# The low levels of a chunked recurrence on halves of the matmul array

## The chip, the cores and the metric

One Trainium2 chip, one core of it. The metric is the device time of one execution in microseconds, the median of several. The core has a matmul engine (TensorE, PE in the profile, with its weight loads as PEld), VectorE (DVE), ScalarE (ACT), GpSimd (POOL) and a DMA-issuing engine (SP). Each works through its own instructions in order and waits on semaphores for the others.

## The reference

One layer of a decoder: 256 tokens, width 1024, all in fp32. A normed input goes through one wide projection into nine parts; two of them feed an attention branch, four a gated linear recurrence (HGRN2), and the branches are merged, followed by cross attention to 256 memory tokens and a feed-forward block. The change lies in the recurrence, which for 8 heads of key width 128 is

```python
qh = silu(heads(q, dk)) * (dk ** -0.5)
fg = lbh + (1.0 - lbh) * sigmoid(heads(f, dk))
kh = 1.0 - fg
...                                    # b = cumsum(log fg) within a chunk
diff = b[:, :, :, None, :] - b[:, :, None, :, :]
decay = where(causal, exp(diff), 0.0)
a = einsum('bhtd,bhsd,bhtsd->bhts', qc, kc, decay)
o = o_inter + einsum('bhts,bhsv->bhtv', a, vc)
```

So for each head a causal 256 x 256 matrix is wanted, whose entry (t, s) is the sum over d of q(t, d) k(s, d) times the product of the forget gates between s and t.

## The kernel before

**Products.** Every large product is made in three parts, hi x hi, hi x lo and lo x hi (L280 to L282). A weight chunk of 1 MB is read by DMA (raw), ScalarE makes hi of it (L211) and VectorE lo = raw - hi (L212). There are three buffers each of hi and lo, and chunks are prepared up to two ahead. `gemm_t` works off two chunks, the two halves of the contraction, for 512 columns; each half takes some 5.5 us of TensorE.

**The recurrence matrix by levels.** For each head and each of two blocks of 128 tokens (16 blocks, index a = 2 x head + block) the kernel keeps the keys `KS[:, a]` and the queries `QP[:, a]`, with the 128 key dimensions on the partitions, and fills the block of the matrix `at3[:, a]` (keys on the partitions, queries along the free axis). This is done level by level: at level L the tokens are seen in groups of 2L, and the later half's queries meet the earlier half's keys. `widen` multiplies queries and keys by the gates of their group, so that they serve the next level. Level one multiplies all keys by the even queries (`QQ`), and a mask leaves the diagonal. Levels 2 and 4 share one product, and so do 8 and 16: `pair_queries` writes the queries in three pieces of 64 into `QQ` (for levels 2 and 4 the fourth piece holds the odd queries), `pair_levels` multiplies all 128 keys by them, and VectorE copies what belongs into `at3` under masks (`lm`). At level 32, 64 and 128 `level` multiplies just the keys and queries that meet. An fp32 product of this kind is one call and two instructions in the trace.

**What sets the order.** TensorE's order is that of the program text. `hgrn` is a generator that is advanced by one `yield` at each tick, and there is a tick after each half of a `gemm_t` or `gemm_f`. So one stretch of recurrence matmuls stands between two halves of a projection: the value projection of the recurrence (`Vb`), that of the attention (`va`), its rotated queries and its rotated keys. The order of VectorE, ScalarE and GpSimd is found by a scheduler when the kernel is built, except for GpSimd's early part, which is in the order of the text. The 16 blocks are handled as two groups g of 8 (heads 0 to 3 and 4 to 7): stretches with 4 blocks each at levels 1 to 16, with 8 each from level 32 on.

**PSUM.** `bank` takes one of four banks of the pool `sm`; the projections take theirs from the four of the pool `mm`. The last step of the query projection (`ev_q`) makes `QQ` for one head at a time: an add and a product on VectorE, Silu on ScalarE (L529) and the copy into `QQ` on ScalarE (L534).

Of the kernel before, what the change touches and what calls it, by code (L numbers as in the profile page):

```python
# [13 lines left out]
AF = mybir.ActivationFunctionType  # L14
ALU = mybir.AluOpType
# [112 lines left out]
def bc(ap, n, axis):  # L128
    shape = list(ap.shape)
    shape.insert(axis, n)  # L130
    return ap.unsqueeze(axis).to_broadcast(shape)


def build(tc, A, out):
    nc = tc.nc
    V, SC, G, PE, SY = nc.vector, nc.scalar, nc.gpsimd, nc.tensor, nc.sync
    with ExitStack() as ctx:
# [11 lines left out]
        def big(tag, name, shape=(128, 8, 256), dt=F32):  # L149
            return bp.tile(list(shape), dt, name=name, tag=tag)  # L150
# [15 lines left out]
        def bank(name, shape=(128, 512)):  # L166
            return sm.tile(list(shape), F32, name=name, tag="sm")
# [3 lines left out]
        lm = cp.tile([128, 448], I32, name="lm")  # L171
# [294 lines left out]
        l0, l1 = gv[:, V_L0:V_L0 + 8], gv[:, V_L1:V_L1 + 8]  # L466
# [13 lines left out]
        QQ = [big(tag, "QQ", (128, 8, 256)) for tag in ("B6", "B6b")]  # L480
# [77 lines left out]
        w = by_k(nxt(), 4)  # L558
# [7 lines left out]
        QP, KS = QK[:, 0], QK[:, 1]  # L566
# [8 lines left out]
        w = by_k(nxt(), 4)  # L575
# [31 lines left out]
        def by_parity(a0, w):  # L607
            return at3[:, a0:a0 + 2].rearrange("p a (j w) -> p a j w", w=2)[:, :, :, w]

        def level_one(g, bs):  # L610
            for b in bs:
                a0 = 8 * g + 2 * b
                ps = bank("l1", (128, 2, 64))
                for j in range(2):
                    PE.matmul(ps[:, j], KS[:, a0 + j], QQ[g][:, a0 + j - 8 * g, 0:64], start=True, stop=True)
                V.tensor_tensor(by_parity(a0, 0), ps, bc(ident2[:, :, 0], 2, 1), op=ALU.mult)

        def widen(g, L, parts="qkt"):
            ga = slice(8 * g, 8 * g + 8)
            T1 = tview(L, g).rearrange("p a (i w) -> p a i w", w=2)  # L620
            T0, Tq = T1[:, :, :, 0], T1[:, :, :, 1]
            if L < 64:
                _, qs = blocks(QP[:, ga], L)
                kf, _ = blocks(KS[:, ga], L)
                n = 64 // L
                if "q" in parts:
                    V.tensor_tensor(qs, qs, T0.unsqueeze(3).to_broadcast([128, 8, n, L]), op=ALU.mult)
                if "k" in parts:
                    V.tensor_tensor(kf, kf, Tq.unsqueeze(3).to_broadcast([128, 8, n, L]), op=ALU.mult)
                if "t" in parts:  # L630
                    G.tensor_tensor(tview(2 * L, g), T0, Tq, op=ALU.mult)
# [22 lines left out]
        def pair_levels(g, L, bs):  # L654
            for b in bs:
                a0 = 8 * g + 2 * b
                n = 256 if L == 2 else 192
                ps = bank("lp", (128, 2, n))
                for j in range(2):
                    PE.matmul(ps[:, j], KS[:, a0 + j], QQ[g][:, a0 + j - 8 * g, 0:n], start=True, stop=True)  # L660
                if L == 2:
                    V.tensor_tensor(by_parity(a0, 1), ps[:, :, 192:256], bc(two_rows, 2, 1), op=ALU.mult)
                for i in range(3):
                    M = L if i == 0 else 2 * L
                    li = (1 if L == 2 else 4) + i
                    mask = lm[:, 64 * li:64 * li + 64].rearrange("p (i j) -> p i j", j=M)
                    V.copy_predicated(blocks(at3[:, a0:a0 + 2], M)[1], bc(mask, 2, 1),
                                      ps[:, :, 64 * i:64 * i + 64].rearrange("p a (i j) -> p a i j", j=M))

        def level(g, M):  # L670
            ga = slice(8 * g, 8 * g + 8)
            if M == 32:
                ps = bank("lv", (128, 8, 32))
                for j in range(8):
                    for w in range(2):
                        r = slice(64 * w, 64 * w + 32)
                        PE.matmul(ps[r, j], KS[:, 8 * g + j, r],
                                  QP[:, 8 * g + j, 64 * w + 32:64 * w + 64], start=True, stop=True)
                for w in range(2):
                    r = slice(64 * w, 64 * w + 32)  # L680
                    V.tensor_copy(at3[r, ga, 64 * w + 32:64 * w + 64], ps[r])
            elif M == 64:
                ps = bank("lv", (128, 8, 64))
                for j in range(8):
                    PE.matmul(ps[0:64, j], KS[:, 8 * g + j, 0:64], QP[:, 8 * g + j, 64:128],
                              start=True, stop=True)
                V.tensor_copy(at3[0:64, ga, 64:128], ps[0:64])
            else:
                ps = bank("lv", (128, 4, 128))
                for j in range(4):  # L690
                    PE.matmul(ps[:, j], KS[:, 8 * g + 2 * j], QP[:, 8 * g + 2 * j + 1],
                              start=True, stop=True)
                SC.activation(AT[:, 16 + 4 * g:20 + 4 * g], ps, AF.Copy)

        def hgrn():
            yield 1
            for g in range(2):
                level_one(g, (0, 1))
                yield 1
                level_one(g, (2, 3))  # L700
                widen(g, 1)
                pair_queries(g, 2)
                yield 1
            for L in (2, 8):
                for g in range(2):
                    pair_levels(g, L, (0, 1))
                    yield 1
                    pair_levels(g, L, (2, 3))
                    widen(g, L, "k")
                    widen(g, 2 * L)  # L710
                    if L == 2:
                        pair_queries(g, 8)
                    yield 1
            for M in (32, 64, 128):
                for g in range(2):
                    level(g, M)
                    if M < 128:
                        widen(g, M)
                    yield 1

        def hgrn_out(obh, obl):
# [359 lines left out]
        for c in range(4):  # L1081
            gemm_f(H1, ev_sum(qxh, qxl, c))
            g = scores(c)
# [219 lines left out]
        for k, u in enumerate(FFN[:-2]):  # L1303
            if u[0] == "I":
                ahead(k)
                w = use(k)
# [14 lines left out]
            w = use(k)  # L1321
# [9 lines left out]
            g, p = u[1:]  # L1331
            a, b = PAIRS[g]
# [6 lines left out]
            if p in (2, 5, 3):  # L1339
                c, op = {2: (1, ALU.add), 5: (7, ALU.subtract), 3: (6, ALU.subtract)}[p]  # L1340
# [25 lines left out]
        n = NF // 2 - 1  # L1366
# [61 lines left out]
        for i in range(2):  # L1428
            a = slice(512 + 256 * i, 768 + 256 * i)
# [47 lines left out]
```

## Time and profile before

| what | value |
|---|---|
| median of 3 runs | 609.9 us (609.57 to 610.69) |
| profiled execution | 610.76 us, span 608.9 us, granted clock 0.997 |
| TensorE busy | 600.3 us (99%) |
| VectorE, ScalarE, GpSimd busy | 452.9, 372.5, 118.3 us |
| recurrence matmuls L615, L660 (two widths) | 4.0, 7.6 and 5.8 us busy |
| recurrence matmuls L677, L685, L691 | 1.4, 2.3 and 2.1 us busy |

The span is the time from the first to the last instruction. Busy time of TensorE contains the tails of matmuls that overlap, so distances between starts say more than durations do. A timeline row gives the start, the length of the group of instructions, the engine, the line, the tiles (out<-in), the shapes and the count. The recurrence's stretches lie between 58 and 176 us.

### The profile page before, as it was taken

Reading aid. Unit: us, or ns where it says so; the run is one execution under the profiler, and the core shown is the slowest. Engines: PE = TensorE matmul, PEld = TensorE weight load, DVE = VectorE, ACT = ScalarE, POOL = GpSimd, SP = SyncE. Lnnn points to the kernel's source line nnn. Section 1 sums busy time; section 2 is a strip of 40 time slices with the busy share of each in tenths; the row PEclk is TensorE's granted clock in tenths of the full one; section 3 lists DMA queues with packets and bytes.
Section 4 is the critical chain, followed back from the end, with each engine's and each line's share of the span. In section 5 each row is a group of like instructions: output and inputs, shape, how many; then the busy total and the mean of one; then the engine's idle time right before and its main releaser. Section 6 shows DMA issues by size and latency. Waiting matters only on the chain.

```text
span 608.9 us, 8359 instructions
## 1 busy us (share of the span) xinstructions
PE 600.3 (99%) x3093; PEld 503.1 (83%) x3093; DVE 452.9 (74%) x749; ACT 372.5 (61%) x600; POOL 118.3 (19%) x136
## 2 busy tenths in 40 slices
PE   8999999999999999999999999999999999999995
PEld 7888888888888888787888888888888888888884
DVE  7679577988756867567967657786789888878863
ACT  7797444433377667646647556684388767676742
POOL 3889200221300250000311432200000000000003
PEclk9999999999999999999999999999999999999998
DMA  8969985793586579777799888782998979796601
GB/s 346 380 213 307 301 288 186 227 343 139 162 255 233 186 229 265 262 305 291 268 249 303 314 256 258 217 337 75 382 284 312 341 279 338 281 341 215 194 1 69
DMA packets 21832, 155.74 MB, mean 256 GB/s; under 512 B 2736, under 2 KB 3376, under 8 KB 5296
## 3 DMA queue, kind: packets, MB, share of 16 engines
q1 hardware_dynamic: 17712, 117.68, 50.7%
q0 software_dynamic: 2880, 20.97, 17.5%
q10 hardware_dynamic: 1200, 16.57, 7.1%
q8 instruction: 24, 0.39, 0.3%
q14 instruction: 16, 0.13, 0.1%
HBM read 154.16 MB, written 32.51 MB: 307 GB/s over the span
## 4 chain that ended last, share of the span: by engine, by line
PE 95%; DMA 2%; DVE 1%; ACT 1%; POOL 0%; issue 0%; POOLq 0%; DVEq 0%; ACTq 0%
PE pst L280 13%; PE pst L282 13%; PE pst L281 13%; PE psf L295 7%; PE bk L282 6%; PE bk L280 6%; PE bk L281 6%; PE psf L296 4%; PE acc L282 3%; PE acc L281 3%; PE acc L280 3%; PE lp L660 2%; DMA raw<-w 2%; PE psg L552 1%; PE pso L282 1%; PE pso L280 1%
## 5 line engine op out<-in xcount | busy, mean ns | idle before, releaser
L212 DVE TENSOR_TENSOR lo<-raw,hi 128x1024 fp32r<-128x1024 f32 (+1 forms) x128 | 154.7, 1225 | 45.1 <-ACT hi L211 43.6
L211 ACT ACTIVATE hi<-raw 128x1024 fp32r<-128x1024 f32 (+1 forms) x128 | 128.6, 1029 | 92.3 <-PE pst L282 51.0
L280 PE MATMUL pst<-hi,Xh 128*128 128x512 f32 x224 | 90.4, 403 | 0.0
L282 PE MATMUL pst<-hi,Xh 128*128 128x512 f32 x224 | 87.5, 390 | 0.0
L281 PE MATMUL pst<-lo,Xh 128*128 128x512 f32 x224 | 87.3, 390 | 0.0
L1182 DVE TENSOR_TENSOR lo<-raw,hi 128x1024 fp32r<-128x1024 f32 x56 | 66.1, 1221 | 12.8 <-ACT hi L1181 12.7
L1181 ACT ACTIVATE hi<-raw 128x1024 fp32r<-128x1024 f32 x56 | 56.3, 1054 | 20.3 <-issue 13.2
L282 PEld LDWEIGHTS pst<-hi,Xh 128*128 128x128 f32 x224 | 42.0, 188 | 9.1
L280 PEld LDWEIGHTS pst<-hi,Xh 128*128 128x128 f32 x224 | 42.1, 188 | 8.5 <-issue 0.3
L281 PEld LDWEIGHTS pst<-lo,Xh 128*128 128x128 f32 x224 | 42.1, 188 | 8.1
L1164 POOL DMA_DIRECT2D raw<-w x5 | 4.5, 892 | 119.2 <-DVE lo L1182 33.7
L280 PE MATMUL acc<-hi,hids 128*128 128x512 f32 x64 | 25.1, 392 | 0.0
L282 PE MATMUL acc<-hi,hids 128*128 128x512 f32 x64 | 24.9, 390 | 0.0
L281 PE MATMUL acc<-lo,hids 128*128 128x512 f32 x64 | 24.9, 389 | 0.0
L280 PE MATMUL bk<-hi,Sh 128*128 128x512 f32 x60 | 23.7, 395 | 0.0
L280 PE MATMUL bk<-hi,h2h 128*128 128x512 f32 x60 | 23.7, 394 | 0.0
L282 PE MATMUL bk<-hi,h2h 128*128 128x512 f32 x60 | 23.4, 390 | 0.0
L282 PE MATMUL bk<-hi,Sh 128*128 128x512 f32 x60 | 23.4, 390 | 0.0
L281 PE MATMUL bk<-lo,h2h 128*128 128x512 f32 x60 | 23.4, 389 | 0.0
L281 PE MATMUL bk<-lo,Sh 128*128 128x512 f32 x60 | 23.3, 389 | 0.0
L295 PE MATMUL psf<-H,hi 128*128 128x512 f32 x64 | 22.8, 400 | 0.0
L295 PE MATMUL psf<-Xh,hi 128*128 128x512 f32 x64 | 22.8, 399 | 0.0
(381 smaller groups left out, 1482.3 us busy)
## 6 DMA issues: line engine op xcount, KB each, us to landing
raw<-w SPq DMA_DIRECT2D x78, 1024.0 KB, 6.2
sum<-w POOLq DMA_DIRECT2D x15, 1024.0 KB, 12.1
raw<-sum SPq DMA_DIRECT2D x13, 1024.0 KB, 6.4
raws<-w SPq DMA_DIRECT2D x11, 1024.0 KB, 5.0
raw<-w POOLq DMA_DIRECT2D x5, 1024.0 KB, 8.2
raw<-w SPq DMA_DIRECT2D x4, 512.0 KB, 6.4
raws<-sum SPq DMA_DIRECT2D x2, 1024.0 KB, 5.2
raw<-w SPq DMA_DIRECT2D x4, 256.0 KB, 3.9
```

The source lines that it names most:

```text
L211: SC.activation(hi[:, a], raw[:, a], AF.Copy)
L212: V.tensor_tensor(lo[:, a], raw[:, a], hi[:, a].bitcast(F32), op=ALU.subtract)
L280: PE.matmul(ps, xh, h, start=first, stop=False, skip_group_check=more)
L281: PE.matmul(ps, xh, l, start=False, stop=False, skip_group_check=more)
L282: PE.matmul(ps, xl, h, start=False, stop=last, skip_group_check=more)
L295: PE.matmul(ps, w[0][:, k, a], X2[:, k], start=k == 0, stop=False)
L296: PE.matmul(ps[:, 0], w[1][:, k, a], X2[:, k, 0], start=False, stop=k == 7)
L552: PE.matmul(pss[c][t], z[:, k, t * 128:(t + 1) * 128], ws[c][0][:, k], start=z is Xh and k == 0, stop=False)
L660: PE.matmul(ps[:, j], KS[:, a0 + j], QQ[g][:, a0 + j - 8 * g, 0:n], start=True, stop=True)
L1164: G.dma_start(raw_of[k], A["w"][AT_CHUNK["I", PAIRS[g][0], 1]], accum_op=ALU.add)
L1181: SC.activation(hi[:, a], raw[:, a], AF.Copy)
L1182: V.tensor_tensor(lo[:, a], raw[:, a], hi[:, a].bitcast(F32), op=ALU.subtract)
```

## The change

Levels 1 to 16 stay within 64 tokens. So the keys are taken in two halves of 64, each multiplied only by the queries of its own half: the first half on the array's columns 0 to 63 (PSUM partitions 0 to 63), the second on columns 64 to 127. The moving operand becomes half as wide (32 for 64, 128 for 256, 96 for 192), the calls twice as many. All 16 blocks of a level go in one stretch: level one fills one PSUM bank, the pair levels fill four. The evictions work on 64 partitions each and are returned as a function that is called per group g, for the second group one tick later. Level 64 puts group 0 on one half of the columns and group 1 on the other; levels 32 and 128 keep their products, both groups in one stretch. The quarter of each block that no masked copy writes any more is zeroed by GpSimd at the start.

```diff
+        halves = (slice(0, 64), slice(64, 128))
+        here = (slice(0, 32), slice(32, 64))
...
-        def level_one(g, bs):
-            for b in bs:
-                a0 = 8 * g + 2 * b
-                ps = bank("l1", (128, 2, 64))
-                for j in range(2):
-                    PE.matmul(ps[:, j], KS[:, a0 + j], QQ[g][:, a0 + j - 8 * g, 0:64], start=True, stop=True)
-                V.tensor_tensor(by_parity(a0, 0), ps, bc(ident2[:, :, 0], 2, 1), op=ALU.mult)
+        def level_one():
+            ps = bank("l1", (128, 16, 32))
+            for a in range(16):
+                for r, c in zip(halves, here):
+                    PE.matmul(ps[r, a], KS[:, a, r], QQ[a // 8][:, a % 8, c], start=True, stop=True)
+
+            def evict(g):
+                ga = slice(8 * g, 8 * g + 8)
+                for r, c in zip(halves, here):
+                    V.tensor_tensor(by_parity(r, ga, 0), ps[r, ga], bc(ident2[r, c, 0], 8, 1), op=ALU.mult)
+            return evict
...
+        def pair_levels(L):
+            n = 4 if L == 2 else 3
+            pss = []
+            for b in range(4):
+                ps = bank("lp", (128, 4, 32 * n))
+                for j in range(4):
+                    a = 4 * b + j
+                    for r, c in zip(halves, here):
+                        q = QQ[a // 8][:, a % 8].rearrange("p (i j) -> p i j", i=4)[:, 0:n, c]
+                        PE.matmul(ps[r, j], KS[:, a, r], q, start=True, stop=True)
+                pss.append(ps)
+
+            def evict(g):
+                for b in (2 * g, 2 * g + 1):
+                    a = slice(4 * b, 4 * b + 4)
+                    for r, c in zip(halves, here):
+                        ps = pss[b][r]
+                        if L == 2:
+                            V.tensor_tensor(by_parity(r, a, 1), ps[:, :, 96:128], bc(two_rows[r, c], 4, 1), op=ALU.mult)
+                        for i in range(3):
...
+                            V.copy_predicated(blocks(at3[r, a, r], M)[1], bc(mask, 4, 1),
+                                              ps[:, :, 32 * i:32 * i + 32].rearrange("p a (i j) -> p a i j", j=M))
+            return evict
...
             elif M == 64:
                 ps = bank("lv", (128, 8, 64))
                 for j in range(8):
-                    PE.matmul(ps[0:64, j], KS[:, 8 * g + j, 0:64], QP[:, 8 * g + j, 64:128],
-                              start=True, stop=True)
-                V.tensor_copy(at3[0:64, ga, 64:128], ps[0:64])
+                    for g, r in enumerate(halves):
+                        a = 8 * g + j
+                        PE.matmul(ps[r, j], KS[:, a, 0:64], QP[:, a, 64:128], start=True, stop=True)
+                for g, r in enumerate(halves):
+                    V.tensor_copy(at3[0:64, 8 * g:8 * g + 8, 64:128], ps[r])
...
         def hgrn():
             yield 1
-            for g in range(2):
-                level_one(g, (0, 1))
+            G.memset(at3[64:128, :, 0:64], 0.0)
+            evict = level_one()
+            evict(0)
+            yield 1
+            widen(0, 1)
+            pair_queries(0, 2)
+            evict(1)
+            yield 1
+            widen(1, 1)
+            pair_queries(1, 2)
+            yield 1
+            yield 1
+            for L in (2, 8):
+                evict = pair_levels(L)
+                evict(0)
                 yield 1
...
```

In the changed file the lines stand lower: L617 is level one's product, L622 its eviction, L670 the product of the pair levels, L679 and L684 their evictions, L634 and L636 the widening of queries and keys, L653 and L656 the query copies of `pair_queries`, L795 the eviction of a projection, L716 the memset.

TensorE at the first tick of the recurrence, before. `pst` is a projection's tile, `l` that of level one:

```order
248 L282 MATMUL pst<-hi,Xh 128x512
249 L615 MATMUL l_736<-QQ,QK 128x64 x2
250 L615 MATMUL l_740<-QQ,QK 128x64 x2
251 L280 MATMUL pst<-hi,Xh 128x512
252 L281 MATMUL pst<-lo,Xh 128x512
```

And after, with the waits of each instruction:

```order
248 L282 MATMUL pst<-hi,Xh 128x512
249 L617 MATMUL l_737<-QQ,QK 64x32 x12
250 L617 MATMUL l_737<-QQ,QK 64x32 [waits Activation_49]
251 L617 MATMUL l_737<-QQ,QK 64x32 x3
252 L617 MATMUL l_737<-QQ,QK 64x32 [waits Activation_49]
253 L617 MATMUL l_737<-QQ,QK 64x32 x3
254 L617 MATMUL l_737<-QQ,QK 64x32 [waits Activation_49]
255 L617 MATMUL l_737<-QQ,QK 64x32 x3
256 L617 MATMUL l_737<-QQ,QK 64x32 [waits Activation_49]
257 L617 MATMUL l_737<-QQ,QK 64x32 x3
258 L617 MATMUL l_737<-QQ,QK 64x32 [waits Activation_49]
259 L617 MATMUL l_737<-QQ,QK 64x32 x3
```

Four products of two heads have become 32 of all eight, and from head 3 on each head's four begin with a wait for ScalarE, which writes `QQ`.

ScalarE at the same place, before:

```order
65 L211 ACTIVATE hi<-raw 128x1024 x2
66 L529 ACTIVATE qt<-qt 128x256
67 L239 DMA sum_0_102<-w 16x16384
68 L534 ACTIVATE QQ<-qt 128x2x2x64
69 L767 ACTIVATE Vb<-pst,r_x 128x512 x2
70 L646 ACTIVATE QQ<-QK 128x8x64
71 L211 ACTIVATE hi<-raw 128x1024
72 L649 ACTIVATE QQ<-QK 128x8x64
```

And after:

```order
65 L211 ACTIVATE hi<-raw 128x1024 x2
66 L529 ACTIVATE qt<-qt 128x256
67 L239 DMA sum_0_102<-w 16x16384
68 L534 ACTIVATE QQ<-qt 128x2x2x64
69 L653 ACTIVATE QQ<-QK 128x8x64 x2
70 L656 ACTIVATE QQ<-QK 128x8x64 x2
71 L795 ACTIVATE Vb<-pst,r_x 128x512 x2
72 L211 ACTIVATE hi<-raw 128x1024 x4
```

Up to the last head's `QQ` (L534) nothing moved; behind it the query copies of both groups now stand ahead of the eviction of `Vb`.

VectorE at the first product of levels 2 and 4, before (`lp` is that product's tile):

```order
90 L662 TENSOR_TENSOR ATS<-lp,two_rows 128x128
91 L212 TENSOR_TENSOR lo<-raw,hi 128x1024
92 L667 COPY_PREDICATED ATS<-lm,lp 128x64x2
93 L662 TENSOR_TENSOR ATS<-lp,two_rows 128x128
94 L667 COPY_PREDICATED ATS<-lm,lp 128x32x4
95 L667 COPY_PREDICATED ATS<-lm,lp 128x64x2
96 L667 COPY_PREDICATED ATS<-lm,lp 128x32x4 x2
97 L212 TENSOR_TENSOR lo<-raw,hi 128x1024
```

And after:

```order
82 L212 TENSOR_TENSOR lo<-raw,hi 128x1024 x6
83 L679 TENSOR_TENSOR ATS<-lp,two_rows 64x4x32
84 L212 TENSOR_TENSOR lo<-raw,hi 128x1024
85 L684 COPY_PREDICATED ATS<-lm,lp 64x4x16x2
86 L679 TENSOR_TENSOR ATS<-lp,two_rows 64x4x32
87 L684 COPY_PREDICATED ATS<-lm,lp 64x4x8x4
88 L684 COPY_PREDICATED ATS<-lm,lp 64x4x16x2
89 L684 COPY_PREDICATED ATS<-lm,lp 64x4x8x4
90 L679 TENSOR_TENSOR ATS<-lp,two_rows 64x4x32
91 L684 COPY_PREDICATED ATS<-lm,lp 64x4x8x4
92 L684 COPY_PREDICATED ATS<-lm,lp 64x4x16x2
```

The lo parts of three chunks come in one row ahead of the evictions, and the evictions of a group then stand nearly together, with fewer lo parts between them. On GpSimd the memset (L716) stands right behind the second of the L410, in the chain of the rotation tables.

More of the change, by code (lines that the diff above doesn't have):

```diff
@@ L605, in build, with by_parity @@
         V.tensor_tensor(two_rows, ident2[:, :, 0], ident2[:, :, 1], op=ALU.add)
-        def by_parity(a0, w):
-            return at3[:, a0:a0 + 2].rearrange("p a (j w) -> p a j w", w=2)[:, :, :, w]
-        def level_one(g, bs):
-            for b in bs:
-                a0 = 8 * g + 2 * b
-                ps = bank("l1", (128, 2, 64))
-                for j in range(2):
-                    PE.matmul(ps[:, j], KS[:, a0 + j], QQ[g][:, a0 + j - 8 * g, 0:64], start=True, stop=True)
-                V.tensor_tensor(by_parity(a0, 0), ps, bc(ident2[:, :, 0], 2, 1), op=ALU.mult)
+        halves = (slice(0, 64), slice(64, 128))
+        here = (slice(0, 32), slice(32, 64))
+        def by_parity(r, a, w):
+            return at3[r, a, r].rearrange("p a (j w) -> p a j w", w=2)[:, :, :, w]
+        def level_one():
[8 more added lines that the diff above has]
+            return evict
         def widen(g, L, parts="qkt"):
@@ L652, in pair_queries @@
                             near.unsqueeze(3).to_broadcast([128, 8, n, 2 * L]), op=ALU.mult)
[L654 to L668, printed above, removed]
@@ L670, in level @@
-        def level(g, M):
-            ga = slice(8 * g, 8 * g + 8)
+        def pair_levels(L):
[17 more added lines that the diff above has]
+                        for i in range(3):
+                            M = L if i == 0 else 2 * L
+                            li = (1 if L == 2 else 4) + i
+                            mask = lm[r, 64 * li + c.start:64 * li + c.stop].rearrange("p (i j) -> p i j", j=M)
+                            V.copy_predicated(blocks(at3[r, a, r], M)[1], bc(mask, 4, 1),
+                                              ps[:, :, 32 * i:32 * i + 32].rearrange("p a (i j) -> p a i j", j=M))
+            return evict
@@ L672, in level @@
+        def level(M):
             if M == 32:
-                ps = bank("lv", (128, 8, 32))
-                for j in range(8):
+                ps = bank("lv", (128, 16, 32))
+                for a in range(16):
                     for w in range(2):
-                        r = slice(64 * w, 64 * w + 32)
-                        PE.matmul(ps[r, j], KS[:, 8 * g + j, r],
-                                  QP[:, 8 * g + j, 64 * w + 32:64 * w + 64], start=True, stop=True)
+                        r, c = slice(64 * w, 64 * w + 32), slice(64 * w + 32, 64 * w + 64)
+                        PE.matmul(ps[r, a], KS[:, a, r], QP[:, a, c], start=True, stop=True)
@@ L679, in level @@
                 for w in range(2):
-                    r = slice(64 * w, 64 * w + 32)
-                    V.tensor_copy(at3[r, ga, 64 * w + 32:64 * w + 64], ps[r])
+                    r, c = slice(64 * w, 64 * w + 32), slice(64 * w + 32, 64 * w + 64)
+                    V.tensor_copy(at3[r, :, c], ps[r])
             elif M == 64:
@@ L684, in level @@
                 for j in range(8):
-                    PE.matmul(ps[0:64, j], KS[:, 8 * g + j, 0:64], QP[:, 8 * g + j, 64:128],
-                              start=True, stop=True)
-                V.tensor_copy(at3[0:64, ga, 64:128], ps[0:64])
-            else:
[L689 to L693, printed above, removed]
+                    for g, r in enumerate(halves):
[3 more added lines that the diff above has]
+                    V.tensor_copy(at3[0:64, 8 * g:8 * g + 8, 64:128], ps[r])
+            else:
+                for g in range(2):
+                    ps = bank("lv", (128, 4, 128))
+                    for j in range(4):
+                        a = 8 * g + 2 * j
+                        PE.matmul(ps[:, j], KS[:, a], QP[:, a + 1], start=True, stop=True)
+                    SC.activation(AT[:, 16 + 4 * g:20 + 4 * g], ps, AF.Copy)
         def hgrn():
             yield 1
-            for g in range(2):
-                level_one(g, (0, 1))
-                yield 1
[L700 to L704, printed above, removed]
+            G.memset(at3[64:128, :, 0:64], 0.0)
[13 more added lines that the diff above has]
+                evict(0)
+                yield 1
                 for g in range(2):
-                    pair_levels(g, L, (0, 1))
-                    yield 1
-                    pair_levels(g, L, (2, 3))
                     widen(g, L, "k")
@@ L712, in hgrn @@
                         pair_queries(g, 8)
+                    if g == 0:
+                        evict(1)
                     yield 1
+                yield 1
             for M in (32, 64, 128):
-                for g in range(2):
-                    level(g, M)
-                    if M < 128:
+                level(M)
+                if M < 128:
+                    for g in range(2):
                         widen(g, M)
+                    yield 1
                     yield 1
```

## The prediction

> **What bounds the kernel now.** I read the page's busy shares and chain first, then the waits of TensorE, then TensorE's timeline around each stretch of recurrence matmuls.
>
> ```profile
> PE 600.3 (99%) x3093; PEld 503.1 (83%) x3093; DVE 452.9 (74%) x749; ACT 372.5 (61%) x600; POOL 118.3 (19%) x136
> PE 95%; DMA 2%; DVE 1%; ACT 1%; POOL 0%; issue 0%; POOLq 0%; DVEq 0%; ACTq 0%
> ```
>
> TensorE works from end to end and carries 95% of the chain that ended last, so a microsecond less of matmul in one stretch is a microsecond less at the end, as long as TensorE then finds its operands ready. The prices come from single stretches. Three of the kinds that the change touches look like this today (level one, levels 2 and 4, levels 8 and 16):
>
> ```profile
> 57.76 0.39 PE L282 MATMUL pst<-hi,Xh 128*128 128x512 f32 x1
> 57.98 1.00 PE L615 MATMUL l<-QQ,QK 128*128 128x64 f32 x8
> 58.79 0.48 PE L280 MATMUL pst<-hi,Xh 128*128 128x512 f32 x1
> 59.11 0.39 PE L281 MATMUL pst<-lo,Xh 128*128 128x512 f32 x1
> ...
> 83.50 1.89 PE L660 MATMUL lp<-QQ,QK 128*128 128x256 f32 x8
> 85.04 0.58 PE L280 MATMUL pst<-hi,Xh 128*128 128x512 f32 x1
> 85.46 0.40 PE L281 MATMUL pst<-lo,Xh 128*128 128x512 f32 x1
> ...
> 112.22 1.46 PE L660 MATMUL lp<-QQ,QK 128*128 128x192 f32 x8
> 113.39 0.53 PE L280 MATMUL pst<-hi,Xh 128*128 128x512 f32 x1
> 113.75 0.40 PE L281 MATMUL pst<-lo,Xh 128*128 128x512 f32 x1
> ```
>
> Columns: start, time to the last end, engine, line, tiles, stationary x moving shape, count. Starts count, not the 0.39: ordinary matmuls start 0.23 us apart (57.76 to 57.98 is 0.22). A stretch costs the start of the following L281, less its own start, less 0.23 for the L280 between. That is 0.90 us for level one, 1.73 for levels 2 and 4 (8 instructions, 0.216 each: each of the four fp32 products of a stretch, two heads by two token blocks, is two instructions in the trace), and 1.30 for levels 8 and 16 (0.163 each). There are four stretches of each: 3.60, 6.92 and 5.20 us.
>
> **Products on half the columns.** Three lines of today's kernel already use part of the array's columns:
>
> ```profile
> 139.92 0.39 PE L282 MATMUL pst<-hi,Xh 128*128 128x512 f32 x1
> 140.24 0.70 PE L677 MATMUL lv<-QK 128*32 128x32 f32 x32
> 140.87 0.50 PE L280 MATMUL pst<-hi,Xh 128*128 128x512 f32 x1
> 141.20 0.39 PE L281 MATMUL pst<-lo,Xh 128*128 128x512 f32 x1
> ...
> 153.39 0.39 PE L282 MATMUL pst<-hi,Xh 128*128 128x512 f32 x1
> 153.71 1.15 PE L685 MATMUL lv<-QK 128*64 128x64 f32 x16
> 154.78 0.50 PE L280 MATMUL pst<-hi,Xh 128*128 128x512 f32 x1
> 155.12 0.39 PE L281 MATMUL pst<-lo,Xh 128*128 128x512 f32 x1
> ...
> 276.07 0.39 PE L282 MATMUL pst<-hi,ob 128*128 128x512 f32 x1
> 276.39 1.52 PE L850 MATMUL ao<-pT,va 128*64 128x256 f32 x16
> 277.84 0.50 PE L280 MATMUL pst<-hi,oah 128*128 128x512 f32 x1
> 278.18 0.40 PE L281 MATMUL pst<-lo,oah 128*128 128x512 f32 x1
> ```
>
> Here the cost runs from the L282 ahead (the array also waits on the way in), less two slots of 0.23: 0.82, 1.27 and 1.65 us. L850 is the model for the change: it alternates between the two column halves, 8 instructions 256 wide and 8 of 128 (two forms under one row). The wide eight alone would take 8 x 0.216 = 1.73 us one after another, and all sixteen took 1.65. L685 is the same shape in one half only: its 16 instructions are (1.15 - 0.22) / 15 = 0.062 us apart (0.22 is one instruction's length), 0.99 for 16, so going into the half-column form and out again costs about 0.3; I take 0.34. Then L850's own matmuls took 1.31 us, four pairs at 0.216 and four at 0.111: two halves in the time of one.
>
> **The sum, part by part.** L670 (levels 2 and 4, all heads): 32 pairs 128 wide at 0.111 plus 0.34 is 3.89 us against 6.92, so 3.02 saved. Levels 8 and 16: 32 pairs 96 wide at half of 0.163, rounded up to 0.083, plus 0.34, is 3.00 against 5.20: 2.20 saved. Level 64: today two stretches of 1.27 in one half; afterwards 16 pairs, which if the halves run together take what 16 single instructions take now, 1.27, so 1.27 saved. Level 32 used two column strips already; joining its two stretches saves one way in and out: the 32 instructions need 0.70 - 0.20 = 0.50 us, so 0.82 + 0.52 = 1.34 against 1.64, 0.30 saved. Level 128 keeps its products: nothing.
>
> Level one is where a new wait comes. By size it would be 32 pairs at 0.062 (the 64-column instructions of L685, since neither narrower width nor pairing shortens the load) plus 0.34: 2.32 against 3.60. But today its first stretch takes only heads 0 and 1, and the change asks for all eight heads at 58 us. The last head's queries are written late, on ScalarE:
>
> ```profile
> 58.18 2.01 ACT L211 ACTIVATE hi<-raw 128x1024 fp32r<-128x1024 f32 x2 [0.15 <-PE pst L282]
> 60.10 0.40 ACT L529 ACTIVATE qt<-qt 128x256 f32<-128x256 f32 x1
> 60.53 0.44 ACT L534 ACTIVATE QQ<-qt 128x256 f32<-128x256 f32 x1
> ```
>
> ScalarE's order up to this L534 is unchanged, and the pair of L211 ahead of it waits for the end of the matmuls just before level one, so head 7's queries land at 60.97 in the changed kernel too. TensorE starts level one at 58.07, has done heads 0 to 6 (28 pairs) at 59.8 and stands for 1.2 us, with the whole next projection queued behind it; four pairs and the way out (0.25) follow. The stretch costs 60.97 + 0.25 + 0.25 - 57.98 = 3.49, and 0.11 of 1.28 is left. Sum: 3.02 + 2.20 + 1.27 + 0.30 + 0.11 = 6.9 us.
>
> **The cover.** VectorE evicts with as many instructions at the levels 2 to 16 (56), on half the partitions and the same 128 elements in each; at level one it has 4 instead of 8.
>
> ```profile
> L667 DVE COPY_PREDICATED ATS<-lm,lp 128x128 f32<-128x128 int32 x48 | 12.9, 322 | 1.4 <-PE lp L660 1.2
> L662 DVE TENSOR_TENSOR ATS<-lp,two_rows 128x128 f32<-128x128 f32 x8 | 2.4, 302 | 4.6 <-PE lp L660 4.6
> L681 DVE COPY ATS<-lv 32x256 f32<-32x256 f32 x4 | 1.7, 417 | 2.4 <-PE lv L677 2.3
> L788 DVE TENSOR_TENSOR rb__1550<-pst,St 128x256 f32<-128x256 f32 x1 | 0.4, 416 | 0.0
> ```
>
> The last two rows say that 32 partitions cost what 128 cost, so I keep 0.31 us each. The load of VectorE in the two stretches of pair levels:
>
> ```profile
> 83.50:112.22 28.72, 28.72 (x129) 24.09 (x128) 23.44 (x52) 13.18 (x17) 0.00 (x0) 1.00 0.60 216
> 112.22:140.15 27.93, 27.93 (x137) 23.86 (x135) 23.19 (x50) 9.01 (x10) 6.85 (x5) 1.00 0.82 270
> ```
>
> Its busy time is the fourth number: 23.44 of 28.72 us and 23.19 of 27.93. TensorE will pass through them in 25.7 each (28.72 - 3.02, 27.93 - 2.20), so 2.3 and 2.5 us remain to spare. That holds: VectorE may run two weight chunks ahead (three buffers of hi and lo). If it does fall behind, the next thing late is lo of a weight chunk or the keys for level 8, and TensorE waits for them. Holding all four small PSUM banks through a tick costs nothing by the order: the next user of that pool comes three projection halves later. Four query copies now stand ahead of the Vb evictions on ScalarE; those banks are wanted again only two projection halves after, some 8 us past the copies.
>
> GpSimd gets a memset in a line that leads to r_x:
>
> ```profile
> 12.76 0.88 DVE L380 SCALAR_TENSOR_TENSOR Xh<-xraw,x0g,Xh 128x256 fp32r<-128x256 f32 x2
> ...
> L631 POOL TENSOR_TENSOR Tt<-fT 128x512 f32<-128x512 f32 x2 | 2.3, 1150 | 0.0
> ...
> 24.37 0.73 POOL L331 TENSOR_TENSOR r_x<-v__336,nhalf 128x2 f32<-128x2 f32 x1 [1.04 <-DVE v__336 L329]
> ...
> 25.40 1.84 ACT L517 ACTIVATE fth<-psg,r_half 128x512 f32<-128x512 f32 x3 [1.31 <-DVE r_half L570]
> ...
> 28.23 0.60 PE L495 MATMUL fT__415<-cst,fth 128*128 128x128 f32 x4
> ```
>
> It can start when the last reader of that buffer is done (13.64), about 0.6 us after its place in the queue. The trace has no large memset: between 0 and 2.3 us (1024 elements, twice L631, which reads two operands besides); I take 1.2. The queue then runs 1.8 late, r_x had 1.04 in hand, and L495 needs the first two of the three L517 (till 26.65) at 28.23, another 1.6. Nothing reaches TensorE; at 2.3 us it would be 0.3.
>
> The Trainium skill says against this change, in "TensorEngine Tiling (Array Packing)", section Key Properties, that changing the tiling mode drains the array. The rows agree: it is the 0.34 us above, which three stretches (levels 1, 2 and 8) pay newly. A kernel to which the rule did not apply would gain 1.0 us more.
>
> **Rivals.** (1) TensorE does not wait at level one: queries come earlier, or the three heads before are slower. The other terms stay: 6.9 + 1.2, 601.8 us. For it speaks little, since L534's time hangs on unchanged work: 7%.
> (2) VectorE becomes the bound in the pair levels. Speaking for it: only 2.3 us to spare, and its evictions now stand in blocks of 16 ahead of lo. If two such waits cost 1 us each, 605: 12%.
> (3) The halves do not share the array. Were a half's weight load not hidden behind the other half's matmul, each pair would be longer by up to 0.062 us (L685's distance bounds it): 5.88, 4.98, 4.31 and 2.32 us for levels 2, 8, 1 and 64, and the sum 1.04 + 0.22 - 0.71 + 0.22 + 0.30 = 1.1: 608.8, within the bound. L850 speaks against it, since its 16 loads left no trace in 1.31 us: 6%. The Trainium skill has this as a rule: "TensorE: Matmul & The Clock Gate", Part 3, says that a weight load overlaps a running matmul only where the row group differs, and here both halves use all rows. The trace disagrees at L850.
> (4) Slower: an eviction of 64 partitions with a pattern one level deeper costs more. It decides from (2.3 + 2.5 + 6.9) / 56 = 0.21 us more on each, so 0.52 instead of 0.31. At twice the price, 56 x 0.31 - 4.8 = 12.6 us of waits, 615.6. L681 against L788 speaks against it: 3%, and 2% for a stall I don't see.
>
> **How the numbers follow.** The profiled execution took 610.8 us (span 608.9), 0.9 above the median 609.9; the gain is taken off the median: 603.0. My forecast has 70%. The range reaches from rival 1 with a little to spare (601.4) past rival 2 and a late memset (606.5); what is left out, rivals 3 and 4, is 11%. A measurement tells 0.2% (1.2 us) from no change: faster 0.89 (forecast, 1 and 2), same 0.06 (3), slower 0.05.
>
> **What would show it.** The stretches in the changed trace: L670 128 wide about 3.5 us from first start to the next L280, 96 wide 2.7, level 64 about 1.1. A gap of some 1.2 us in level one that ends with ACT L534 near 61 us. No wait of TensorE for L212 between 84 and 140. I am wrong if L670's starts come singly 0.11 us apart instead of in pairs, if L684 is longer than 0.5 us, or if waits for lo appear.

## The result and the profile after

The changed kernel takes 603.75 us (median of 4 runs, 601.98 to 604.15) against 609.74 (609.18 to 610.69) of the kernel before in the same comparison: a ratio of 0.989, interval 0.9875 to 0.991. The profiled execution took 603.53 us with a span of 601.8, against 610.8 and 608.9 before. The forecast was 603.0 us. The total is close; one of its terms is not, and gains that were not forecast hide part of it in the profile.

The page of the changed kernel, busy shares, granted clock and chain:

```profile
PE 592.1 (98%) x3189; PEld 495.4 (82%) x3189; DVE 458.8 (76%) x743; ACT 372.4 (62%) x600; POOL 121.9 (20%) x137
PEclk9999899999999999999999999999999999999999
PE 96%; DVE 1%; ACT 1%; DMA 1%; issue 0%; POOL 0%; POOLq 0%; DVEq 0%; ACTq 0%
```

TensorE is still the chain. Its clock shows an 8 in the fifth slice (60 to 75 us). TensorE's longest wait behind the warm-up (engine, tile, line, what it waits for: us in total, times, longest):

```profile
PE l L617 <- ACT QQ L534: 1.1, 1, 1.1
```

It is the forecast wait; there is none for L212 between 84 and 140 us. TensorE's timeline of the stretches that the prediction priced (start, time to the last end, engine, line, tiles, shapes, count, wait): levels 2 and 4, levels 8 and 16, level 32, level 64.

```profile
84.25 0.39 PE L282 MATMUL pst<-hi,Xh 128*128 128x512 f32 x1
84.57 3.71 PE L670 MATMUL lp<-QQ,QK 128*64 128x128 f32 x64
...
88.55 0.40 PE L281 MATMUL pst<-lo,Xh 128*128 128x512 f32 x1
...
109.88 0.39 PE L282 MATMUL pst<-hi,Xh 128*128 128x512 f32 x1
110.20 2.86 PE L670 MATMUL lp<-QQ,QK 128*64 128x96 f32 x64
...
113.33 0.40 PE L281 MATMUL pst<-lo,Xh 128*128 128x512 f32 x1
...
135.86 1.21 PE L694 MATMUL lv<-QK 128*32 128x32 f32 x64
...
149.01 1.15 PE L703 MATMUL lv<-QK 128*64 128x64 f32 x32
```

Measured from the start of the L282 ahead to the L281 behind (135.54 to 137.33 and 148.69 to 150.43 us for the last two), less two slots of 0.23, they cost 3.84, 2.99, 1.33 and 1.28 us; the forecast was 3.89, 3.00, 1.34 and 1.27. Level 64 shows the sharing most plainly: 32 instructions in 1.15 us, where the kernel before needed 1.15 for 16. The two starts of a pair are 0.006 us apart; the pairs follow each other every 0.109 us at levels 2 and 4 and every 0.058 us at level 64.

TensorE's timeline at level one, where the sum went wrong:

```profile
57.72 1.82 PE L617 MATMUL l<-QQ,QK 128*64 128x32 f32 x56
60.66 0.61 PE L617 MATMUL l<-QQ,QK 128*64 128x32 f32 x8 [1.11 <-ACT QQ L534]
61.20 0.80 PE L280 MATMUL pst<-hi,Xh 128*128 128x512 f32 x1
61.80 0.63 PE L281 MATMUL pst<-lo,Xh 128*128 128x512 f32 x1
62.22 0.63 PE L282 MATMUL pst<-hi,Xh 128*128 128x512 f32 x1
...
63.93 0.50 PE L280 MATMUL pst<-hi,Xh 128*128 128x512 f32 x1
64.26 0.39 PE L281 MATMUL pst<-lo,Xh 128*128 128x512 f32 x1
```

The wait is there, 1.11 us, ended by L534. But the projection's matmuls behind it start 0.43 us apart instead of 0.23 until 63.93. Against full rate that is 0.60 - 0.33 for the first step, 5 x 0.20 and 0.33 - 0.23 for the last: about 1.4 us that nobody forecast. Busy time by windows of the trace, with the granted clock as the third number from the end:

```profile
57.31:60.72 3.41, 2.30 (x61) 1.84 (x61) 3.41 (x6) 3.31 (x8) 3.28 (x4) 1.00 1.02 195
60.72:64.14 3.42, 3.42 (x15) 2.78 (x16) 3.38 (x6) 1.12 (x2) 3.42 (x5) 0.50 1.42 479
```

The clock is at full speed in the first and at one half through the second, 3.41 us; by the trace's record of the clock it is at full speed again from 64.14.

Where the time went, by how much earlier each projection matmul starts than its like in the profile before, read where that lead stays level between two stretches: 0.35 ahead at 57 us, 0.98 behind at 83 (level one done): level one lost 1.33. Then the levels 2 and 4 bring 3.09, 8 and 16 bring 2.26, level 32 brings 0.32, levels 64 and 128 bring 1.45: 6.1 ahead at 178 us. The first 0.35 is luck of the two executions: the clock goes to full speed at 7.42 us in the profile before and at 6.11 in this one, and up to there the first matmuls start 0.43 us apart instead of 0.23. A last 1.1 comes in cross attention, 0.9 of it between 403.6 and 405.0 us, where the profile before had a wait for VectorE that is now gone:

```profile
404.75 0.38 PE L277 MATMUL xo<-ph,vxl 128*128 128x256 f32 x1 [0.29 <-DVE vxl L325]
```

That row is of the kernel before. Its wait is 0.29 us; the rest of the 0.9 are slow starts beside it for which the profile names no wait. Together this is 7.2 us, against 7.1 between the two spans.

### The profile page after: what moved, and what is told of

Its sections match the earlier page's. It is cut to its first block, busy times and chain, and to the rows that moved or that the text cites. A ratio compares the mean times of both kernels' runs of the same rounds, so it can differ in the third digit from the quotient of the medians.

```text
span 601.8 us, 8522 instructions
## 1 busy us (share of the span) xinstructions
PE 592.1 (98%) x3189; PEld 495.4 (82%) x3189; DVE 458.8 (76%) x743; ACT 372.4 (62%) x600; POOL 121.9 (20%) x137
## 4 chain that ended last, share of the span: by engine, by line
PE 96%; DVE 1%; ACT 1%; DMA 1%; issue 0%; POOL 0%; POOLq 0%; DVEq 0%; ACTq 0%
PE pst L280 13%; PE pst L282 13%; PE pst L281 13%; PE psf L295 7%; PE bk L282 6%; PE bk L280 6%; PE bk L281 6%; PE psf L296 4%; PE acc L282 3%; PE acc L280 3%; PE acc L281 3%; PE psg L552 1%; PE pso L282 1%; PE pso L280 1%; PE pso L281 1%; PE lp L670 1%
## 5 line engine op out<-in xcount | busy, mean ns | idle before, releaser
L212 DVE TENSOR_TENSOR lo<-raw,hi 128x1024 fp32r<-128x1024 f32 (+1 forms) x128 | 158.4, 1255 | 46.9 <-ACT hi L211 45.0
L282 PE MATMUL pst<-hi,Xh 128*128 128x512 f32 x224 | 87.8, 392 | 0.0
L281 PE MATMUL pst<-lo,Xh 128*128 128x512 f32 x224 | 87.8, 392 | 0.0
L282 PEld LDWEIGHTS pst<-hi,Xh 128*128 128x128 f32 x224 | 42.3, 189 | 9.1
L281 PEld LDWEIGHTS pst<-lo,Xh 128*128 128x128 f32 x224 | 42.5, 190 | 8.3
L282 PE MATMUL acc<-hi,hids 128*128 128x512 f32 x64 | 24.9, 390 | 0.0
L281 PE MATMUL acc<-lo,hids 128*128 128x512 f32 x64 | 24.9, 389 | 0.0
L282 PE MATMUL bk<-hi,Sh 128*128 128x512 f32 x60 | 23.4, 390 | 0.0
L282 PE MATMUL bk<-hi,h2h 128*128 128x512 f32 x60 | 23.4, 390 | 0.0
L281 PE MATMUL bk<-lo,Sh 128*128 128x512 f32 x60 | 23.4, 389 | 0.0
L281 PE MATMUL bk<-lo,h2h 128*128 128x512 f32 x60 | 23.3, 389 | 0.0
```

Source lines behind the costliest of these rows:

```text
L212: V.tensor_tensor(lo[:, a], raw[:, a], hi[:, a].bitcast(F32), op=ALU.subtract)
L281: PE.matmul(ps, xh, l, start=False, stop=False, skip_group_check=more)
L282: PE.matmul(ps, xl, h, start=False, stop=last, skip_group_check=more)
```

## The experiments

| version | median us | range | ratio to the kernel before (interval) |
|---|---|---|---|
| changed kernel again | 603.69 | 601.79 to 604.05 | 0.9887 (0.9865 to 0.9908) |
| level one as before, rest changed | 601.91 | 601.69 to 602.81 | 0.987 (0.9849 to 0.9891) |
| wait filled by eight products | 602.39 | 601.74 to 602.85 | 0.9874 (0.9854 to 0.9895) |
| wait part filled by three | 602.29 | 601.95 to 602.71 | 0.9872 (0.9855 to 0.989) |
| level one a tick later | 601.49 | 600.58 to 601.92 | 0.9856 (0.9831 to 0.988) |
| the same, idle tick kept | 600.27 | 600.23 to 601.17 | 0.9842 (0.9825 to 0.986) |
| halves of a bank one after the other | 605.04 | 603.58 to 605.52 | 0.992 (0.9899 to 0.994) |
| kernel before, with a wait | 612.22 | 611.84 to 612.95 | 1.0034 (1.002 to 1.0047) |

The theory after the first result: level one waits for ScalarE as forecast, and the wait, by leaving TensorE idle, brings half a clock behind it. Rivals: the narrow products themselves or the change of tiling bring it; or it is chance of one execution.

**The changed kernel again.**

> The changed kernel once more, for a second profile and an interval on the same chip as the next three. If the matmuls at half rate behind level one come from the wait, they are there again: 6 to 7 of them 0.43 us apart, about 1.4 us lost. If they were an accident of the one profiled execution, they are gone and the time is near 602.

The wait is again 1.11 us, and half rate again follows, 8 matmuls long this time, by TensorE's timeline:

```profile
61.17 0.43 PE L617 MATMUL l<-QQ,QK 128*64 128x32 f32 x8 [1.11 <-ACT QQ L534]
61.53 0.64 PE L280 MATMUL pst<-hi,Xh 128*128 128x512 f32 x1
61.97 0.63 PE L281 MATMUL pst<-lo,Xh 128*128 128x512 f32 x1
...
64.96 0.48 PE L282 MATMUL pst<-hi,Xh 128*128 128x512 f32 x1
```

The clock was at one half from 61.73 to 65.14, so 3.41 us again, but it fell 0.56 us after the wait was over, with TensorE working. It does not follow the wait directly. The nine times of the changed kernel in both comparisons also fall into two groups, 601.79 to 602.23 (three) and 603.53 to 604.15 (six), 1.8 us apart in their means.

**Level one as it was, the rest changed.** `level_one` gives way to the old four stretches of wide products:

```
-            evict = level_one()
-            evict(0)
-            yield 1
-            widen(0, 1)
...
+            for g in range(2):
+                level_one_old(g, (0, 1))
+                yield 1
+                level_one_old(g, (2, 3))
+                widen(g, 1)
+                pair_queries(g, 2)
+                yield 1
```

> Level one as before the change (four stretches over four ticks, all 128 columns, 0.90 us each), the pair levels and level 64 as changed. If the pair levels and above bring what their stretches show (3.1 + 2.2 + 0.3 + 1.3 = 6.9 us), this kernel is 6.9 us faster than the one before, near 602.9, and about 1 to 1.5 us faster than the changed kernel, because neither the wait nor the half rate occurs. Rival: the narrow products of the pair levels also slow the clock; then matmuls 0.43 us apart stand behind L670's line.

No wait, no half rate, and 1.8 us faster than the whole change on the same chip. So level one's part of the change, as it stands, costs time by the medians, where the prediction gave it a gain of 0.11. Against the three shorter times of the changed kernel (601.79 to 602.23) it costs next to nothing.

**The wait filled.** Ahead of head 7's products stand eight products that nobody reads:

```
+            fill = bank("fill", (128, 256))
...
+                if a == 14:
+                    for k in range(8):
+                        PE.matmul(fill, Xh[:, k, 0:128], Xh[:, k], start=True, stop=True)
```

> The changed kernel with eight matmuls that nothing reads (128x256, fp32r) ahead of head 7's products in level one, so that the array works during most of the wait. If idleness makes the clock fall, the wait stays about as long in time (head 7's queries land no earlier), but the matmuls behind it run 0.23 us apart: about 1.4 us faster than the changed kernel, some 602.4. If the half rate comes from the narrow products or the change of tiling, it is still there and the time is the same or 0.3 us longer.

TensorE's timeline there:

```profile
59.76 1.22 PE L619 MATMUL fill<-Xh 128*128 128x256 f32 x8
60.95 0.42 PE L621 MATMUL l<-QQ,QK 128*64 128x32 f32 x8
61.31 0.50 PE L280 MATMUL pst<-hi,Xh 128*128 128x512 f32 x1
61.64 0.40 PE L281 MATMUL pst<-lo,Xh 128*128 128x512 f32 x1
```

Head 7's products start when their queries are there, as before, but what follows them is at full rate, and the kernel is 1.3 us faster. The same narrow products and the same change of tiling are there, so in this execution they don't bring the half rate by themselves. This is useless work that shortens the kernel.

**The wait part filled.** Three such products instead of eight.

> The changed kernel with three unread 128 x 256 products ahead of head 7's instead of eight: by 1.22 us for eight they take 0.46 us and leave a wait of about 0.65 us instead of 1.11. If any wait of this place brings the half rate, the products behind it are 0.43 us apart for about 3 us and the time is the changed kernel's 603.7; if it needs a wait of about 1 us, the products are at 0.23 us at once and the time is that of eight, 602.4.

TensorE's timeline at the same place:

```profile
61.18 0.42 PE L621 MATMUL l<-QQ,QK 128*64 128x32 f32 x8 [0.57 <-ACT QQ L534]
61.54 0.50 PE L280 MATMUL pst<-hi,Xh 128*128 128x512 f32 x1
61.88 0.40 PE L281 MATMUL pst<-lo,Xh 128*128 128x512 f32 x1
```

A wait of 0.57 us is left and no half rate follows. It is as good as eight: of the eight times of the two versions none is in the slower group (602.85 is the longest), where six of the nine of the changed kernel are.

**The kernel before, with a wait.** One extra product in its first level-one stretch reads head 7's queries:

```
+                if g == 0:
+                    extra_one = bank("x1", (128, 64))
+                    PE.matmul(extra_one, KS[:, 15], QQ[1][:, 7, 0:64], start=True, stop=True)
```

> The kernel before, with one product more at the start of its first level-one stretch that reads head 7's queries and whose result is not used: TensorE waits there for the same copy of ScalarE near 61 us, behind wide products and with no narrow product and no half-column tiling around it. The first stretch stands near 58.8 us, so the wait is about 2 us. If a wait alone brings the half rate, the products behind it are 0.43 us apart for about 3 us and the time is 609.7 + 2 + 1.4 = 613.1; if the narrow products or the half-column tiling ahead of the wait are needed, they are 0.23 apart at once and it is 611.8.

TensorE's timeline there:

```profile
60.29 0.69 PE L701 MATMUL x<-QQ,QK 128*128 128x64 f32 x2 [2.03 <-ACT QQ L534]
60.74 0.77 PE L280 MATMUL pst<-hi,Xh 128*128 128x512 f32 x1
61.31 0.63 PE L281 MATMUL pst<-lo,Xh 128*128 128x512 f32 x1
...
63.44 0.50 PE L280 MATMUL pst<-hi,Xh 128*128 128x512 f32 x1
```

Half rate follows here as well, in full-column tiling and behind eight instructions of 64, so half columns are not needed for it. The clock stood at one half from 60.25 to 63.66. The median of 612.22 lies between the two expected times, and the profiled execution (612.95) near the upper. The spans differ by only 2.2 us though the place itself cost 4.0 (the lead over the profile before goes from 0.72 us ahead to 3.30 behind): the 0.72 ahead is again the clock, which rose at 5.63 us here, and 1.1 comes back in cross attention, because the wait for vxl at 404 us is gone in this trace too. That wait, then, is no gift of the change: it goes away in a kernel whose cross attention is that of before.

**Two halves of a bank one after the other.** The order of the pair levels' products is turned:

```
-                for j in range(4):
-                    a = 4 * b + j
-                    for r, c in zip(halves, here):
+                for r, c in zip(halves, here):
+                    for j in range(4):
+                        a = 4 * b + j
```

> The products of the pair levels are issued in another order only: within each bank first the four products of one half of the array's columns, then the four of the other half, where the changed kernel alternates between the halves. If two halves overlap only when neighbours in the order lie on different halves, three of four neighbours no longer do: a stretch of L670 goes from 3.84 us back towards the 6.92 us of the kernel before (levels 2 and 4) and from 2.99 towards 5.20 (levels 8 and 16), by three quarters of the gain 2.3 and 1.7 us, and the kernel takes about 607.5 us. Rival: TensorE looks further ahead than one instruction, or the halves save time for another reason (half the columns to load for each product); then the stretches stay at 3.84 and 2.99 and the time at 603.7.

TensorE's timeline at the two kinds of stretches:

```profile
83.08 4.54 PE L670 MATMUL lp<-QQ,QK 128*64 128x128 f32 x64
...
87.89 0.39 PE L281 MATMUL pst<-lo,Xh 128*128 128x512 f32 x1
...
109.54 3.58 PE L670 MATMUL lp<-QQ,QK 128*64 128x96 f32 x64
...
113.39 0.39 PE L281 MATMUL pst<-lo,Xh 128*128 128x512 f32 x1
```

Neither expectation holds. The stretches cost 4.67 and 3.71 us, 0.83 and 0.72 more than in alternation, not 2.3 and 1.7 and not nothing (from the L282 ahead, at 82.76 and 109.22, as above). The single starts in the trace show why. At 128 wide, a group of eight instructions (one half of a bank) takes its 0.109 us each, and a new group begins every 0.494 us, when the fifth of the group ahead starts. I read this so: the other half's instructions begin beside the last four of the half in front (its first at 0.494 us, ahead of the sixth of the half in front at 0.597): order matters, but only beyond four instructions or so. That the gain comes from two halves at work at once is shown by it, since 64 instructions one after another at 0.109 would be 7.0 us; having half the columns to load saves nothing by itself, since products 128 wide on all columns (L691 of the kernel before) start 0.111 us apart.

This run also tells what the half rate hangs on, since its level one is that of the changed kernel (TensorE's timeline):

```profile
60.72 0.42 PE L617 MATMUL l<-QQ,QK 128*64 128x32 f32 x8 [1.11 <-ACT QQ L534]
61.07 0.50 PE L280 MATMUL pst<-hi,Xh 128*128 128x512 f32 x1
61.41 0.40 PE L281 MATMUL pst<-lo,Xh 128*128 128x512 f32 x1
```

The same wait of 1.11 us, and no half rate. The clock's record explains the difference. In the changed kernel it goes to full speed at 6.11 us, in the first projection behind the warm-up products, and stays for 54.61 us, which is 16 x 3.413, then half for 3.41. In the repeat it is the same from 7.12 us, and in all ten traces the time from one change of the clock to the next is a whole multiple of 3.413 us. So the clock is decided at a fixed beat. The first rise lies between 4.41 and 7.46 us in the ten traces, so which of the windows catches the idle time is chance. With the beat counted on from the first rise (4.75 us here), two windows of this run, with the same columns as above, are:

```profile
55.95:59.36 3.41, 3.41 (x63) 2.82 (x63) 3.41 (x6) 3.33 (x7) 3.29 (x4) 1.00 0.84 219
59.36:62.78 3.42, 2.31 (x25) 1.86 (x22) 3.42 (x5) 1.85 (x4) 3.42 (x3) 1.00 1.02 218
```

Here the boundary at 59.36 parts the two: 54 of the 56 narrow instructions start in the window ahead, and the whole wait lies behind it, with the last two of them, head 7's eight and the wide ones from 61.07 on. In the changed kernel's 57.31 to 60.72 all 56 and the wait are in one window, and the next has half the clock; so it is in the repeat (58.32 to 61.73). The wait without the 56 brought no drop here; nor did narrow products without a wait, which the version with level one a tick later (below) has all 64 in one window, with the beat counted on in the same way:

```profile
62.43:65.85 3.42, 3.42 (x71) 2.86 (x71) 1.19 (x4) 2.49 (x4) 1.50 (x5) 1.00 1.10 419
```

So the rival of chance was half right: the wait is in every profiled execution of the changed kernel, the drop falls where the beat puts wait and narrow products into one window. The kernel before with a wait of 2.03 us needed no narrow products for it; its window, 56.83 to 60.24, had TensorE busy for 1.43 us.

The beat also says which of the filled versions is a test of the drop. In the profile with eight products a window ends at 59.87 us, behind the start of the last of the 56 (59.60), so the wait would have lain in the window after them, as in the run just shown, and by that run half rate was not to be expected even without the filling. With three products most of the 56 and what is left of the wait do lie in one window, the clock at full speed in it and after it:

```profile
58.66:62.07 3.41, 2.84 (x63) 2.51 (x60) 3.38 (x5) 3.01 (x5) 3.41 (x3) 1.00 0.95 192
```

That filling brings the drop to an end rests on this window and on the eight times, not on the profile with eight products.

The mean granted clock of every execution bears on the two groups of times of the changed kernel. One window of 3.41 us at half takes 0.5 x 3.41 / 602 = 0.003 off it, and a fall at the end of a program can take as much. The three of the faster group had 0.999, which leaves no room for a drop; five of the six of the slower group had 0.993 to 0.996, the two profiled ones with the drop among them. The sixth, 604.15 us, had 0.999: it was slow without a drop, and why is open. In the kernel before with a wait the times do not part by the clock: 611.84 us came with 0.996, and 612.31 with 0.999.

**Level one a tick later.** It then finds all queries written; the idle tick ahead of level two is dropped so that the rest stays in place:

```
+            yield 1
             evict = level_one()
...
             pair_queries(1, 2)
             yield 1
-            yield 1
```

> Level one one tick later, in place of one of the two idle ticks before the pair levels. By my theory the wait for head 7's queries (1.1 us) goes, and with it the matmuls at half rate (1.4 us): the stretch of level one falls from 3.93 to about 2.3 us, and the time by about 2.8 us against the changed kernel, near 601. Rival: the half rate comes from the thin products of level one themselves or from the change of tiling; then it stays, and only about 1.5 us are gained. A second rival: the pair levels now wait for queries that are one tick later; then a wait of TensorE stands at L670 and the gain is smaller.

TensorE's timeline at level one, and at the one wait behind it:

```profile
62.93 0.39 PE L282 MATMUL pst<-hi,Xh 128*128 128x512 f32 x1
63.25 2.06 PE L617 MATMUL l<-QQ,QK 128*64 128x32 f32 x64
...
65.57 0.39 PE L281 MATMUL pst<-lo,Xh 128*128 128x512 f32 x1
...
102.54 0.50 PE L281 MATMUL pst<-lo,Xh 128*128 128x512 f32 x1 [0.27 <-DVE lo L212]
```

Without the wait level one costs 2.18 us, against the 2.32 worked out and 3.60 before: the full gain is to be had. The version is 2.2 us faster than the change, and not the 2.8 expected, in part at least because a weight chunk now comes late (the last row, a wait of 0.27 us): VectorE falls behind, as rival 2 had it, in a small form. With one tick less ahead of the pair levels, VectorE's work of level one and theirs press together.

**The same with the idle tick kept.** One more `yield 1` ahead of the loop over the pair levels.

> Level one a tick later, as in the version with 601.5 us, but the idle tick ahead of level two is kept, so that levels 2 to 128 stand a tick later than there. In that version the crowded VectorE delivered a weight chunk late (wait of 0.3 us for L212 near 102 us and two slow rows behind it, about 0.8 us in all). If the dropped idle tick was the cause, that wait is gone and the time is about 600.7 us; if VectorE is behind by its work in the pair levels themselves, the wait only moves a tick later and the time stays at 601.5; if the end of level 128 then comes late for its readers near 176 us, a new wait stands there and the time is above 601.5.

600.27 us, the best of all: by the two ratios to the kernel before, which were taken in different comparisons, 2.7 us below the changed kernel's repeat. Against the version without the idle tick it is 0.9 us by the ratios, and their intervals overlap; that the late chunk is gone is shown by the trace. TensorE's list of waits, complete, has none for L212 and none in level one:

```profile
PE warm L371 <- DVE still L368: 1.6, 1, 1.6
PE xT L1106 <- DVE xp L1100: 0.2, 1, 0.2
PE psg L552 <- ACT hi L211: 0.2, 1, 0.2
```

## Why the prediction was right, and where it was not

- **The pair levels, 32 and 64: right.** All four stretches are within 0.05 us of their price, and the price of two halves taken from L850 held at widths where no row had shown it. The runs show alternation as the reason (halves in groups of eight lose 0.83 and 0.72). By stretch the savings are 3.08, 2.21, 0.31 and 1.26. By position they are 3.09, 2.26, 0.32 and 1.45; 0.18 of the last lies behind level 64, between 163 and 178 us, where the prediction put level 128 at nothing, and I have not assigned it.
- **The mode change, 0.34 us:** held with every stretch whose total depended on it. The prediction chose it where L685 gave 0.28; the stretches give 3.84 - 32 x 0.109 = 0.35 at levels 2 and 4 and 1.28 - 16 x 0.058 = 0.35 at level 64. The rule on draining in the Trainium skill, "TensorEngine Tiling (Array Packing)", section Key Properties, agrees with it.
- **Rival 3, no sharing, is false**, and with it the rule of the Trainium skill, "TensorE: Matmul & The Clock Gate", Part 3, for this case: the 128 weight loads at the two pair levels, on the same rows in both halves, add nothing to pairs of 0.109 us.
- **Rival 4 is false, rival 2 nearly so.** Evictions cost what they did, by the group of the changed kernel (mean 320 ns, forecast 0.31 us):

```profile
L684 DVE COPY_PREDICATED ATS<-lm,lp 64x128 f32<-64x128 int32 x48 | 14.4, 320 | 1.1 <-PE lp L670 0.3
```

  But VectorE was busier there than forecast (fourth number, its busy time in the two stretches of pair levels):

```profile
84.57:110.20 25.63, 25.63 (x162) 21.42 (x161) 24.00 (x51) 12.66 (x16) 0.00 (x0) 1.00 0.53 189
110.20:135.86 25.66, 25.66 (x169) 21.44 (x168) 24.74 (x49) 9.01 (x10) 6.81 (x4) 1.00 0.72 274
```

  24.0 and 24.7 of 25.6 us leave 1.6 and 0.9 to spare, not 2.3 and 2.5. No wait came of it in the changed kernel; one tick less was enough for one.
- **The memset: harmless**, as said, and cheaper: 0.95 us against 1.2, by GpSimd's timeline; r_x came 0.24 us later.

```profile
13.66 0.95 POOL L716 MEMSET ATS<- 64x1024 f32 x1 [0.75 <-POOL rt L410]
```

- **The step that failed is level one.** The wait itself was right to 0.1 us, in its cause and place. What I left out is what a wait does to the matmuls behind it: I charged 1.2 us of idle time and nothing after. Where the drop falls, the term is not +0.11 but -1.33, of which half rate is 1.4. By the medians filling the wait brought 1.3 us back, keeping the old level one 1.8.
- **The total came out near the forecast because of two gains that I did not have either**, and that is luck: 0.35 us ahead of level one, from an earlier rise of the clock, and 1.1 about the wait for vxl, which only the profile before has. Both are differences of the two executions that were compared, not gains of the change. By the medians the gain is 6.0 us, 0.9 short of 6.9.
- **Rival 1** (no wait at level one, 601.8) was priced without half rate; made real, it gave 600.27.

## What to carry to other kernels

Two halves of the array's columns do two narrow products in the time of one if the halves alternate in the order of issue; price such a stretch by the spacing of single instructions that the trace already has, plus once the way in and out. When a stretch is gathered at an earlier point, look for its last operand's writer: a wait of 1.1 us cost up to 2.5. Moving the stretch to where its operands are ready, and keeping the gap behind it that lets VectorE catch up, was worth 2.7 us more than the change as made.

## What was not expected of the hardware

TensorE's clock fell to one half for one window of 3.41 us after a window in which TensorE was busy 2.30 of 3.41 us by the row above, with 56 narrow instructions among it; a wait of 1.11 us among wide matmuls, at 2.31 busy, did not bring it. Busy time as the profile has it is thus not by itself what decides the clock. In the kernel before with a wait of 2.03 us the drop had the same length (60.25 to 63.66).

The Trainium skill, "TensorE: Matmul & The Clock Gate", Part 1, gives a free-running window of 3413 ns and half the clock after an idle one. The length and the free running agree with the traces, at 3.41 us and 54.61 = 16 x 3.413. That the window must be idle doesn't: in the changed kernel's the idle part was 1.11 us. What activity decides is open, and no kernel was run that sets the wait at a chosen point of the window.

One count does part the windows of this case. Add up the moving columns of the matmuls that start in a window (512 for a wide one, 32 for a narrow one), for each of the some 1,750 windows of the ten traces. Every window followed by half the clock had at most 2,496: 1,024 in the kernel before with a wait, 2,368 and 2,496 in the changed kernel and its repeat, the rest at the ends of the programs. Every window followed by full speed had at least 2,816: 3,904 with the wait among wide matmuls, and 3,392 with three filling products, 768 of them theirs. This is an estimate from the starts and shapes of the timelines, made after all runs; another weight (the columns of the array in use, say) parts the windows too, and no run was made to tell them apart.
